# Softmax cross-entropy over 1 GB of logits: label logits picked out of the loaded tiles instead of gathered from memory

## The chip, the cores and the metric

The kernel runs on one core of one Trainium2 chip. The metric is the device time of one execution in microseconds, the median of several runs.

## The reference

```python
batch, seq, vocab = 16, 512, 32000          # logits float32, labels int32

def reference(logits, labels):
    logits_max = np.max(logits, axis=-1, keepdims=True)
    log_sum_exp = np.log(np.sum(np.exp(logits - logits_max), axis=-1)) + logits_max.squeeze(-1)
    log_probs = logits - log_sum_exp[..., np.newaxis]
    return -log_probs[np.arange(batch)[:, None], np.arange(seq), labels]
```

The loss of a row is log(sum(exp(row))) minus the row's logit at its label. The logits are 8192 rows of 32000 values, 1048.6 MB. All must be read once. From each row one single value, the label's logit, is needed besides the sum.

## The kernel before

The rows are laid out as 128 partitions times 64 groups, so one group is one row on each partition. Each group is loaded as two tiles of 128x16000 (8.2 MB each) into three rotating buffers. ScalarE (ACT) takes the exponential in place and sums it on the way. The label logits come by 64 indirect gathers, each fetching one 4-byte value per partition straight from HBM. GpSimd (POOL) issues them all at the start.

```python
    nc.gpsimd.iota(idx[:], pattern=[[V, G]], base=0, channel_multiplier=G * V)
    nc.gpsimd.tensor_tensor(out=idx[:], in0=idx[:], in1=labs32, op=ALU.add)
    for g in range(G):                      # G = 64
        nc.gpsimd.indirect_dma_start(
            out=lab_logit[:, g:g + 1], out_offset=None, in_=lg,
            in_offset=bass.IndirectOffsetOnAxis(ap=idx[:, g:g + 1], axis=1),
        )
    # ... (exp(g, ap): nc.scalar.activation(out=ap, in_=ap, func=EXP, accum_out=...))
    for j, (g, b, at, n) in enumerate(loads):
        if b not in buffers:
            buffers[b] = data.tile([P, W], FP32, tag="t", name="t")   # pool of 3 buffers, W = 16000
        t = buffers[b]
        # ...
        nc.sync.dma_start(out=t[:, at:at + n], in_=lg_pg[:, g, c0:c0 + n])
        exp(g, t[:, at:at + n])
        # ... (near the end: reduce the sums, logarithm, subtract lab_logit)
```

The first group and the last two are cut into smaller loads, so that the start and the end of the run are short.

The softmax here doesn't subtract the row's maximum and nothing guards it: scores larger than these inputs give would overflow.

Of the kernel before, what the change touches and what calls it, by code (L numbers as in the profile page):

```python
# [1 line left out]

# [5 lines left out]

FP32 = mybir.dt.float32  # L10
I32 = mybir.dt.int32


EXP = mybir.ActivationFunctionType.Exp
LN = mybir.ActivationFunctionType.Ln
ALU = mybir.AluOpType
X = mybir.AxisListType.X


@with_exitstack  # L20
def kernel(
    ctx: ExitStack,
    tc: tile.TileContext,
    logits: bass.AP,
    labels: bass.AP,
    out: bass.AP,
):
    nc = tc.nc

    B, S, V = logits.shape  # L30
    P = 128
    G = B * S // P
    W = 16000


    lg = logits.rearrange("b s v -> (b s) v")
    lg_pg = lg.rearrange("(p g) v -> p g v", g=G)
    labels_pg = labels.rearrange("b s -> (b s)").rearrange("(p g) -> p g", g=G)
    out_pg = out.rearrange("b s -> (b s)").rearrange("(p g) -> p g", g=G)



    loads = []

    def plan(g, widths_by_buffer, order):

        n_buffers = 1 + max((l[1] for l in loads), default=-1)
        for b, i in order:
            ws = widths_by_buffer[b]
            loads.append((g, n_buffers + b, sum(ws[:i]), ws[i]))  # L50

    plan(0, [[4000, 4000, 8000], [16000]], [(0, 0), (0, 1), (0, 2), (1, 0)])
    for g in range(1, G - 2):
        plan(g, [[W], [W]], [(0, 0), (1, 0)])
    plan(G - 2, [[W], [10000, 6000]], [(0, 0), (1, 0), (1, 1)])
    plan(
        G - 1,
        [[7400, 5840, 2260], [4540, 3720, 2920, 1780, 1460, 1120], [960]],
        [(0, 0), (0, 1), (1, 0), (1, 1), (1, 2), (0, 2), (1, 3), (1, 4), (1, 5), (2, 0)],
    )  # L60
    assert sum(l[3] for l in loads) == G * V

    data = ctx.enter_context(tc.tile_pool(name="data", bufs=3))
    persist = ctx.enter_context(tc.tile_pool(name="persist", bufs=1))

    labs64 = persist.tile([P, G], mybir.dt.int64)
    labs32 = labs64[:].bitcast(I32).rearrange("p (g two) -> p g two", two=2)[:, :, 0]
    idx = persist.tile([P, G], I32)
    lab_logit = persist.tile([P, G], FP32)
    K = 10  # L70
    sums = persist.tile([P, G - 1, 5], FP32)
    sums_last = persist.tile([P, K], FP32)
    totals = persist.tile([P, G - 1], FP32)
    logsum = persist.tile([P, G - 1], FP32)
    res = persist.tile([P, G - 1], FP32)
    part = persist.tile([P, 1], FP32)
    logsum_last = persist.tile([P, 1], FP32)
    res_last = persist.tile([P, 1], FP32)

    ctx.enter_context(tc.manual_schedule())  # L80


    nc.scalar.dma_start(out=labs64[:], in_=labels_pg)
    nc.scalar.preload_act_table_set("natural_log_exp_and_others")  # L84
    nc.vector.memset(sums[:], 0.0)  # L85
    nc.gpsimd.iota(idx[:], pattern=[[V, G]], base=0, channel_multiplier=G * V)  # L86
    nc.gpsimd.tensor_tensor(out=idx[:], in0=idx[:], in1=labs32, op=ALU.add)  # L87
    for g in range(G):
        nc.gpsimd.indirect_dma_start(  # L89
            out=lab_logit[:, g:g + 1],  # L90
            out_offset=None,
            in_=lg,
            in_offset=bass.IndirectOffsetOnAxis(ap=idx[:, g:g + 1], axis=1),
        )


    buffers = {}
    col = {}
    n_exp = {}

    def exp(g, ap):
        k = n_exp.get(g, 0)
        n_exp[g] = k + 1
        s = sums[:, g, k:k + 1] if g < G - 1 else sums_last[:, k:k + 1]
        nc.scalar.activation(out=ap, in_=ap, func=EXP, accum_out=s)  # L105

    for j, (g, b, at, n) in enumerate(loads):
        if b not in buffers:
            buffers[b] = data.tile([P, W], FP32, tag="t", name="t")
        t = buffers[b]  # L110
        c0 = col.get(g, 0)
        col[g] = c0 + n
        nc.sync.dma_start(out=t[:, at:at + n], in_=lg_pg[:, g, c0:c0 + n])  # L113
        exp(g, t[:, at:at + n])

        left = len(loads) - 1 - j
        if left == 6:
            nc.vector.reduce_sum(out=totals[:], in_=sums[:], axis=X)  # L118
        if left == 4:
            nc.scalar.activation(out=logsum[:], in_=totals[:], func=LN)  # L120
            nc.vector.tensor_tensor(out=res[:], in0=logsum[:], in1=lab_logit[:, 0:G - 1], op=ALU.subtract)  # L121
        if left == 1:
            nc.vector.reduce_sum(out=part[:], in_=sums_last[:, 0:K - 1], axis=X)  # L123
    assert n_exp[G - 1] == K
    nc.sync.dma_start(out=out_pg[:, 0:G - 1], in_=res[:])

    nc.scalar.activation(out=logsum_last[:], in_=sums_last[:, K - 1:K], func=LN, bias=part[:])  # L127
    nc.vector.tensor_tensor(out=res_last[:], in0=logsum_last[:], in1=lab_logit[:, G - 1:G], op=ALU.subtract)  # L128
    nc.sync.dma_start(out=out_pg[:, G - 1:G], in_=res_last[:])


# [1 line left out]
_INS = ['logits', 'labels']  # L133
_OUTS = [((16, 512), 'float32')]


# [23 lines left out]
```

## Time and profile before

| what | value |
|---|---|
| time, median of 3 runs | 2435.71 us |
| span of the profiled run | 2434.1 us |
| ACT busy | 1748.9 us (72%) |
| HBM read, mean rate | 1048.67 MB, 431 GB/s |
| full exp (128x16000) | 13.54 us |
| load of a full tile, issue to landing (median) | 43.0 us |

First, from the page: busy tenths and transfer rate in 40 slices of some 61 us, then the chain of waits.

```profile
ACT  4777766777677776777677776777667776777769
POOL 3222000000000000000000000000000000000000
DMA  9999999999999999999999999999999999999998
GB/s 421 422 421 433 425 438 431 427 438 438 433 426 436 438 434 426 435 438 434 426 435 436 435 430 431 436 435 430 431 436 438 431 427 436 438 433 426 438 433 377
...
DMA 76%; ACT 24%; issue 0%; SPq 0%; ACTq 0%; DVE 0%
```

The DMA engines are full from start to end, and nothing else is. POOL is busy only in the first four slices, where the gathers are. The chain is loads and, between them, the exps that free their buffers. The page's table of queues shows the two kinds of traffic; the columns are packets, MB and the share of the 16 engines' time. Below it is the page's line for the loads of full tiles, which ends with the median time from issue to landing (from the load's DMA instruction to the arrival of its last byte):

```profile
q1 hardware_dynamic: 20304, 1048.62, 99.8%
q0 software_dynamic: 2048, 0.04, 0.1%
...
t<-in_logits_dram SPq DMA_DIRECT2D x124, 8000.0 KB, 43.0
```

By its own time the gathers' queue (q0) seems not worth a thought. The windows view, by stretch of the run, shows more. Its columns are the stretch's length, the busy times of VectorE (DVE), ACT and POOL with instruction counts, the clock, the DMA share and the rate:

```profile
0.00:60.00 60.00, 0.32 (x1) 29.13 (x9) 19.68 (x26) 1.00 0.98 411
60.00:240.00 180.00, 0.00 (x0) 127.72 (x19) 39.44 (x42) 1.00 1.01 427
480.00:1200.00 720.00, 0.00 (x0) 517.89 (x76) 0.00 (x0) 1.00 1.00 433
```

While POOL issues gathers the loads move at 427 GB/s, afterwards at 433. The timeline shows the same in the starts of exps, first among gathers and then after them (start, duration, instruction, what ended the idle time before):

```profile
61.53 13.54 ACT L105 ACTIVATE t<-t 128x16000 f32<-128x16000 f32 x1 [5.79 <-DMA t<-in_logits_dram]
61.59 0.94 POOL L89 DMA_INDIRECT lab_logit<-in_logits_dram,idx  x1 [1.80 <-DMA lab_logit<-in_logits_dram,idx]
...
80.69 13.54 ACT L105 ACTIVATE t<-t 128x16000 f32<-128x16000 f32 x1 [5.52 <-DMA t<-in_logits_dram]
...
100.10 13.54 ACT L105 ACTIVATE t<-t 128x16000 f32<-128x16000 f32 x1 [5.78 <-DMA t<-in_logits_dram]
...
991.68 13.54 ACT L105 ACTIVATE t<-t 128x16000 f32<-128x16000 f32 x1 [5.27 <-DMA t<-in_logits_dram]
...
1010.60 13.54 ACT L105 ACTIVATE t<-t 128x16000 f32<-128x16000 f32 x1 [5.29 <-DMA t<-in_logits_dram]
```

Among gathers the exps start 19.16 and 19.41 us apart, later 18.92 us in the two lines shown and 18.89 to 18.91 us nearly everywhere. Each waits for its load, so these distances are the time of a load.

### The profile page before, as it was taken

To read this page: it belongs to the slowest core of one execution; us is meant where nothing else is said; L and a number is where in the kernel's file an instruction comes from. 1 tells how busy PE (TensorE), PEld (TensorE's weight loads), DVE (VectorE), ACT (ScalarE), POOL (GpSimd) and SP (SyncE) were. 2 spreads that over 40 slices of the span, in tenths; PEclk is the share of its full clock that TensorE was granted. 3 is DMA by queue.
4 is the path that set the end of the run, shared out by engine and by line. 5 is a ranking of instruction groups with operands and counts; after the bars stand their busy time and mean duration, and the time that the engine had idled before them with its cause. 6 is when DMAs were issued, how large, how long until landed. Compare 5 with 4: busy or idle time off the path is not lost.

```text
span 2434.1 us, 807 instructions
## 1 busy us (share of the span) xinstructions
DVE 1.3 (0%) x5; ACT 1748.9 (72%) x281; POOL 61.0 (3%) x70
## 2 busy tenths in 40 slices
DVE  0000000000000000000000000000000000000000
ACT  4777766777677776777677776777667776777769
POOL 3222000000000000000000000000000000000000
DMA  9999999999999999999999999999999999999998
GB/s 421 422 421 433 425 438 431 427 438 438 433 426 436 438 434 426 435 438 434 426 435 436 435 430 431 436 435 430 431 436 438 431 427 436 438 433 426 438 433 377
DMA packets 22502, 1048.77 MB, mean 431 GB/s; under 512 B 4576, under 2 KB 4704, under 8 KB 5216
## 3 DMA queue, kind: packets, MB, share of 16 engines
q1 hardware_dynamic: 20304, 1048.62, 99.8%
q0 software_dynamic: 2048, 0.04, 0.1%
q10 hardware_dynamic: 144, 0.07, 0.0%
q14 instruction: 6, 0.05, 0.0%
HBM read 1048.67 MB, written 0.03 MB: 431 GB/s over the span
## 4 chain that ended last, share of the span: by engine, by line
DMA 76%; ACT 24%; issue 0%; SPq 0%; ACTq 0%; DVE 0%
DMA t<-in_logits_dram 76%; ACT t L105 24%; SPq L113 0%; ACTq L105 0%; ACT logsum_last L127 0%; DVE res_last L128 0%; ACT logsum L120 0%
## 5 line engine op out<-in xcount | busy, mean ns | idle before, releaser
L105 ACT ACTIVATE t<-t 128x16000 f32<-128x16000 f32 (+5 forms) x139 | 1734.8, 12481 | 681.4 <-DMA t<-in_logits_dram 681.2
L89 POOL DMA_INDIRECT lab_logit<-in_logits_dram,idx x64 | 60.3, 942 | 178.3 <-DMA lab_logit<-in_logits_dram,idx 174.5
L105 ACT ACTIVATION_READ_ACCUMULATOR t<-t 128x1 f32 x139 | 25.9, 186 | 0.0
L84 ACT ACT_TABLE_LOAD x1 | 1.3, 1283 | 1.2 <-PEq L144 1.2
L118 DVE TENSOR_REDUCE totals<-sums 128x63 f32<-128x315 f32 x1 | 0.5, 480 | 2398.9 <-ACT t L105 2398.9
L87 POOL TENSOR_TENSOR idx<-idx,labs 128x64 int32<-128x64 int32 x1 | 0.3, 322 | 7.5 <-DMA labs<-in_labels_dram 7.5
L85 DVE MEMSET sums<- 128x315 f32 x1 | 0.3, 321 | 0.9 <-PEq L144 0.9
L127 ACT ACTIVATE logsum_last<-sums_last,part 128x1 f32<-128x1 f32 x1 | 0.3, 294 | 0.0
L121 DVE TENSOR_TENSOR res<-logsum,lab_logit 128x63 f32<-128x63 f32 x1 | 0.2, 225 | 25.3 <-ACT logsum L120 25.3
L120 ACT ACTIVATE logsum<-totals 128x63 f32<-128x63 f32 x1 | 0.2, 238 | 0.0
L86 POOL IOTA idx<- 128x64 int32 x1 | 0.2, 172 | 0.4 <-PEq L155 0.4
L123 DVE TENSOR_REDUCE part<-sums_last 128x1 f32<-128x9 f32 x1 | 0.2, 163 | 4.0 <-ACT t L105 4.0
L128 DVE TENSOR_TENSOR res_last<-logsum_last,lab_logit 128x1 f32<-128x1 f32 x1 | 0.2, 159 | 1.2 <-ACT logsum_last L127 1.2
L144 POOL MEMSET const-uint8-127<- 128x1 uint8 x1 | 0.1, 118 | 0.0
L144 POOL MEMSET const-bfloat16-1.0<- 128x1 bf16 x1 | 0.1, 113 | 0.0
L144 POOL MEMSET const-float32-0.0<- 128x1 f32 x1 | 0.1, 98 | 0.2 <-issue 0.2
L144 POOL MEMSET const-float32-1.0<- 128x1 f32 x1 | 0.1, 104 | 0.0
## 6 DMA issues: line engine op xcount, KB each, us to landing
t<-in_logits_dram SPq DMA_DIRECT2D x124, 8000.0 KB, 43.0
t<-in_logits_dram SPq DMA_DIRECT2D x1, 5000.0 KB, 35.9
t<-in_logits_dram SPq DMA_DIRECT2D x2, 2000.0 KB, 9.6
t<-in_logits_dram SPq DMA_DIRECT2D x1, 4000.0 KB, 21.4
t<-in_logits_dram SPq DMA_DIRECT2D x1, 3700.0 KB, 32.9
t<-in_logits_dram SPq DMA_DIRECT2D x1, 3000.0 KB, 42.6
t<-in_logits_dram SPq DMA_DIRECT2D x1, 2920.0 KB, 39.5
t<-in_logits_dram SPq DMA_DIRECT2D x1, 2270.0 KB, 26.4
```

Of the source, the lines that this page charges most:

```text
L84: nc.scalar.preload_act_table_set("natural_log_exp_and_others")
L85: nc.vector.memset(sums[:], 0.0)
L86: nc.gpsimd.iota(idx[:], pattern=[[V, G]], base=0, channel_multiplier=G * V)
L87: nc.gpsimd.tensor_tensor(out=idx[:], in0=idx[:], in1=labs32, op=ALU.add)
L89: nc.gpsimd.indirect_dma_start(out=lab_logit[:, g:g + 1], out_offset=None, in_=lg, in_offset=bass.IndirectOffsetOnAxis(ap=idx[:, g:g + 1], ...
L105: nc.scalar.activation(out=ap, in_=ap, func=EXP, accum_out=s)
L118: nc.vector.reduce_sum(out=totals[:], in_=sums[:], axis=X)
L120: nc.scalar.activation(out=logsum[:], in_=totals[:], func=LN)
L121: nc.vector.tensor_tensor(out=res[:], in0=logsum[:], in1=lab_logit[:, 0:G - 1], op=ALU.subtract)
L123: nc.vector.reduce_sum(out=part[:], in_=sums_last[:, 0:K - 1], axis=X)
L127: nc.scalar.activation(out=logsum_last[:], in_=sums_last[:, K - 1:K], func=LN, bias=part[:])
L144: nc = _bacc.Bacc("TRN2", target_bir_lowering=False, num_devices=1)
```

## The change

The intent: the label's logit passes through on-chip memory anyway with its tile, so it need not be fetched a second time. POOL's indexed copy takes 48 entries per tile out of it before the exp overwrites it. It returns 16 values on each partition for each column of its index list (3 columns and 48 values here). The program takes them as the picks of 16 neighbouring partitions, and VectorE sorts out each partition's own with a one-hot mask, four groups at a time. Groups 0, 61, 62 and 63 keep their gathers, three of them because their loads are cut in pieces.

```diff
+    gathered = [0, G - 3, G - 2, G - 1]
+    picked = [g for g in range(G) if g not in gathered]
-    for g in range(G):
+    for g in gathered:
         nc.gpsimd.indirect_dma_start(
 # ... about 25 small VectorE operations that make index lists and the one-hot mask, once
         nc.sync.dma_start(out=t[:, at:at + n], in_=lg_pg[:, g, c0:c0 + n])
+        if g in picked:
+            # ... (h: which half of the row; i: place in the batch of NB = 4; pk: tile of 128 x 8 x 48)
+            nc.gpsimd.indirect_copy(
+                out=pk[:, 2 * i + h, :], data=t[:], idxs=lists[:, g, h, 0:3], i_know_this_is_slow=True
+            )
         exp(g, t[:, at:at + n])
+        if g in picked and h == 1 and i == NB - 1:
+            nc.vector.copy_predicated(own[:], one_hot[:].unsqueeze(1).to_broadcast([P, NB * 2, NI]), pk[:])
+            nc.vector.reduce_sum(out=found[...], in_=own[...], axis=X)   # shortened
 # ... near the end: choose the half that holds the label, into lab_logit
```

More of the change, by code (lines that the diff above doesn't have):

```diff
@@ L64 @@
     persist = ctx.enter_context(tc.tile_pool(name="persist", bufs=1))
+    NI = 48
+    gathered = [0, G - 3, G - 2, G - 1]
+    picked = [g for g in range(G) if g not in gathered]
+    NB = 4
+    assert len(picked) % NB == 0
     labs64 = persist.tile([P, G], mybir.dt.int64)
@@ L69 @@
     lab_logit = persist.tile([P, G], FP32)
+    part16 = persist.tile([P, 1], I32)
+    part16f = persist.tile([P, 1], FP32)
+    mine = persist.tile([P, 3], FP32)
+    mine_at = persist.tile([P, 3], FP32)
+    at_entry = persist.tile([P, 1], FP32)
+    entries = persist.tile([P, NI], FP32)
+    one_hot = persist.tile([P, NI], mybir.dt.int32)
+    clamped = persist.tile([P, 2, G], FP32)
+    lists = persist.tile([P, G, 2, 4], mybir.dt.uint16)
+    own = persist.tile([P, NB * 2, NI], FP32)
+    found = persist.tile([P, 2, G], FP32)
+    in_first = persist.tile([P, G], mybir.dt.int32)
+    picks = ctx.enter_context(tc.tile_pool(name="picks", bufs=2))
     K = 10
@@ L87 @@
     nc.gpsimd.tensor_tensor(out=idx[:], in0=idx[:], in1=labs32, op=ALU.add)
-    for g in range(G):
+    nc.gpsimd.iota(part16[:], pattern=[[0, 1]], base=0, channel_multiplier=1)
+    nc.gpsimd.iota(entries[:], pattern=[[1, NI]], base=0, channel_multiplier=0, allow_small_or_imprecise_dtypes=True)
+    for g in gathered:
         nc.gpsimd.indirect_dma_start(
@@ L94 @@
         )
+    nc.vector.tensor_single_scalar(out=part16[:], in_=part16[:], scalar=15, op=ALU.bitwise_and)
+    nc.vector.tensor_copy(out=part16f[:], in_=part16[:])
+    for q in range(3):
+        nc.vector.tensor_scalar(
+            out=mine[:, q:q + 1], in0=part16f[:], scalar1=4.0 * q, scalar2=None, op0=ALU.add
+        )
+    for n in (12.0, 6.0):
+        nc.vector.tensor_scalar(
+            out=mine_at[:], in0=mine[:], scalar1=n, scalar2=n, op0=ALU.is_ge, op1=ALU.mult
+        )
+        nc.vector.tensor_tensor(out=mine[:], in0=mine[:], in1=mine_at[:], op=ALU.subtract)
+    nc.vector.tensor_scalar(out=mine[:], in0=mine[:], scalar1=4.0, scalar2=None, op0=ALU.is_ge)
+    for q in range(3):
+        nc.vector.tensor_scalar(
+            out=mine_at[:, q:q + 1], in0=mine[:, q:q + 1], scalar1=16.0 * q, scalar2=None, op0=ALU.mult
+        )
+    nc.vector.reduce_sum(out=at_entry[:], in_=mine_at[:], axis=X)
+    nc.vector.tensor_tensor(out=at_entry[:], in0=at_entry[:], in1=part16f[:], op=ALU.add)
+    nc.vector.tensor_scalar(
+        out=one_hot[:], in0=entries[:], scalar1=at_entry[:], scalar2=None, op0=ALU.is_equal
+    )
+    nc.vector.tensor_scalar(
+        out=clamped[:, 0, :], in0=labs32, scalar1=float(W - 1), scalar2=None, op0=ALU.min
+    )
+    nc.vector.tensor_scalar(
+        out=clamped[:, 1, :], in0=labs32, scalar1=float(-W), scalar2=0.0, op0=ALU.add, op1=ALU.max
+    )
+    nc.vector.tensor_scalar(
+        out=in_first[:], in0=labs32, scalar1=float(W), scalar2=None, op0=ALU.is_lt
+    )
+    for h in range(2):
+        for q in range(3):
+            nc.vector.tensor_scalar(
+                out=lists[:, :, h, q], in0=clamped[:, h, :], scalar1=mine[:, q:q + 1], scalar2=None, op0=ALU.mult
+            )
+    nc.vector.memset(own[:], 0.0)
     buffers = {}
@@ L113 @@
         nc.sync.dma_start(out=t[:, at:at + n], in_=lg_pg[:, g, c0:c0 + n])
-        exp(g, t[:, at:at + n])
+        if g in picked:
+            h = c0 // W
+            i = picked.index(g) % NB
+            if h == 0 and i == 0:
+                pk = picks.tile([P, NB * 2, NI], FP32, tag="pk", name="pk")
+            nc.gpsimd.indirect_copy(
+                out=pk[:, 2 * i + h, :], data=t[:], idxs=lists[:, g, h, 0:3], i_know_this_is_slow=True
+            )
+        exp(g, t[:, at:at + n])
+        if g in picked and h == 1 and i == NB - 1:
+            nc.vector.copy_predicated(own[:], one_hot[:].unsqueeze(1).to_broadcast([P, NB * 2, NI]), pk[:])
+            nc.vector.reduce_sum(
+                out=found[:, :, g - NB + 1:g + 1].rearrange("p h g -> p g h"),
+                in_=own[:].rearrange("p (g h) n -> p g h n", h=2),
+                axis=X,
+            )
         left = len(loads) - 1 - j
@@ L118 @@
             nc.vector.reduce_sum(out=totals[:], in_=sums[:], axis=X)
+            lo, hi = picked[0], picked[-1] + 1
+            nc.vector.tensor_copy(out=lab_logit[:, lo:hi], in_=found[:, 1, lo:hi])
+            nc.vector.copy_predicated(lab_logit[:, lo:hi], in_first[:, lo:hi], found[:, 0, lo:hi])
         if left == 4:
```

## The prediction

> **What bounds the kernel now.** The loads. The page shows DMA busy in every slice but the last at 9 tenths or more, 431 GB/s over the span; the windows view from 480 us on shows 433 GB/s. The chain of waits is 76% DMA of t and 24% exp. [...] ACT is busy 72%: an exp of 128x16000 takes 13.54 us, and in the timeline those start 18.90 us apart once things are steady, each waiting about 5.4 us for its load. A load lands 43.0 us after issue (median): 18.9 us of its own and about 24 us queued behind others.
>
> **What the change removes.** 60 of 64 indirect gathers. They run from 9 to 247 us on POOL, off the chain, but share the DMA engines: while they run, the twelve full exps after 42.1 us start 19.04 to 19.42 us apart, 231.2 us in all against 12 x 18.90 = 226.8 us, so 4.4 us lost. The first exp of a full tile, at 42.12 us, is by the same rate some 0.8 us late (first quarter tile landed at 8.3 us, started about 3.5 us, plus 37.8 us). Together about 5.2 us; 60/64 of it is about 4.9 us. This is the only gain, since the loads are unchanged.
>
> **What it adds.** (a) 120 indexed copies on POOL, each between the landing of a tile and its in-place exp. The trace has none. [...] (b) About 25 small VectorE operations once, 15 pairs of predicated copy and reduction (128x384, an estimate of 0.5 to 1 us each, from 0.48 us for the 128x315 reduction in this trace), and two at the end. All hide: VectorE is idle.
>
> **On the critical path?** The copy lengthens landing-to-release from 13.7 to 13.7 + x us, so the next load is issued x later and its queued time falls from 24 to 24 - x us. While x stays under roughly 18 us (and POOL under 18.9 us a tile) the DMA always holds another load and nothing is lost. [...] The last three groups are gathered, so the tail is as before.
>
> **Prediction.** 2435.7 - 4.9 = 2430.8 us; I say 2431, 2429 to 2434.5 with 8 in 10. Chances: faster by over 2% 0.01, within 2% 0.92, slower by over 2% 0.07.
>
> **What would show each step.** Right: exps start 18.90 us apart from about 60 us on instead of from 260 us; first slices at about 433 GB/s instead of 421; median issue-to-landing 43 minus x; the last 35 us unchanged; software DMA packets a sixteenth. Exps wait for POOL, not DMA.
>
> **What would make it wrong.** An indexed copy of over 18 us: POOL or the exchange of three buffers then paces the loads, and every microsecond over that costs about 120 us in all (at 25 us POOL alone needs 3000 us). A copy near 15 us would leave little queued and expose late engines, costing tenths of a microsecond per tile. The gathers' 19.3 us spacing may partly be a start-up effect unrelated to them; then the gain is under 4.9 us.

The sum of the forecast is 2435.7 - 4.9 = 2430.8 us, put as 2431 us; it had no term for a pick. x is the time of a pick, and "roughly 18 us" is the estimate, set below the 24 us that a load queues. The "late engines" have this ground in the trace of the kernel before: the 16 landings recorded for each full load lie 0.6 to 2.4 us apart (median 1.3 us). That they would cost tenths of a microsecond per tile was a guess, which runs below test.

## The result

The changed kernel takes 2431.28 us (median of 4 runs, 2431.22 to 2431.33), the kernel before beside it 2435.61 us. The ratio is 0.9982, with a 95% interval of 0.9965 to 0.9999. The outputs are right. The change is a gain of 4.3 us. The span of the profiled run fell from 2434.1 to 2429.5 us, by 4.6 us.

The page after, the same lines:

```profile
ACT  4777767777677767777677776777667776777769
POOL 0000000000000000000000000000000000000000
DMA  9999999999999999999999999999999999999998
GB/s 423 438 423 437 438 428 432 438 436 424 438 436 428 434 438 433 427 438 435 429 434 437 433 428 437 435 427 435 437 434 429 435 437 426 435 437 433 430 434 377
...
q1 hardware_dynamic: 20304, 1048.62, 99.8%
...
q0 software_dynamic: 128, 0.00, 0.0%
...
DMA 73%; ACT 24%; issue 2%; POOL 1%; SPq 0%; POOLq 0%; DVE 0%; ACTq 0%
```

The gathers' queue is down to a sixteenth. A single slice of the GB/s row says little, since all slices but the last scatter between 423 and 438. The windows view averages enough to see it:

```profile
0.00:60.00 60.00, 4.35 (x27) 29.13 (x9) 5.04 (x12) 1.00 1.00 427
60.00:240.00 180.00, 1.15 (x2) 130.55 (x19) 6.81 (x10) 1.00 1.00 433
480.00:1200.00 720.00, 5.74 (x10) 519.06 (x77) 25.82 (x38) 1.00 1.00 434
```

The stretch from 60 to 240 us now has the rate of the rest of the run, 433 GB/s. The timeline after has the pick between landing and exp:

```profile
61.36 0.69 POOL L182 INDIRECT_COPY pk<-t,lists 128x48 f32 x1 [46.96 <-DMA t<-in_logits_dram]
62.08 13.54 ACT L168 ACTIVATE t<-t 128x16000 f32<-128x16000 f32 x1 [6.81 <-POOL pk L182]
...
80.24 0.69 POOL L182 INDIRECT_COPY pk<-t,lists 128x48 f32 x1 [18.20 <-DMA t<-in_logits_dram]
80.96 13.54 ACT L168 ACTIVATE t<-t 128x16000 f32<-128x16000 f32 x1 [5.25 <-POOL pk L182]
...
99.79 13.54 ACT L168 ACTIVATE t<-t 128x16000 f32<-128x16000 f32 x1 [5.20 <-POOL pk L182]
```

The exps start 18.88 and 18.83 us apart here, without the slow start. They wait for POOL now, but ACT's wait before each exp is no longer than it was later in the run before. The page's groups of new work (busy time, mean ns of one) and its first line of DMA issues:

```profile
L182 POOL INDIRECT_COPY pk<-t,lists 128x48 f32 x120 | 81.6, 680 | 2216.8 <-DMA t<-in_logits_dram 2216.8
L187 DVE COPY_PREDICATED own<-one_hot,pk 128x384 f32<-128x384 int32 x15 | 8.9, 593 | 2282.9 <-POOL pk L182 2282.9
...
L188 DVE TENSOR_REDUCE found<-own 128x8 f32<-128x384 f32 x15 | 8.3, 555 | 0.5
...
t<-in_logits_dram SPq DMA_DIRECT2D x124, 8000.0 KB, 41.6
```

Issue to landing is 41.6 us, where it was 43.0: the loads are issued 1.4 us later and spend that much less time queued. The pick therefore lengthens the path from landing to release by 1.4 us, twice the 0.68 us that its line shows. This will matter below.

Where the gain lies can be read from the starts of corresponding exps in the two timelines. Exp 4 (the first full tile, no pick in front of it) starts at 42.12 us before and 41.64 us after, 0.48 us earlier. Exp 18 starts at 311.24 and 307.71 us, 3.53 us earlier though it now has a pick of about 1.4 us in front, so its tile landed some 4.9 us earlier. From there on nothing more is gained: exp 125, the first without a pick again, starts at 2334.94 and 2330.34 us, 4.60 us earlier. Between them one lone spacing of 19.24 us (exp 21 to 22), which the kernel before has not in that place, gives back 0.3 us. To the end the difference stays 4.6 us, so the tail is as it was.

### The profile page after: what moved, and what is told of

Same layout as the page of the kernel before. It is cut to its first block, busy times and chain, and to the rows that moved or that the text cites. A ratio compares the mean times of both kernels' runs of the same rounds, so it can differ in the third digit from the quotient of the medians. Undisturbed runs are those within 1.5% of the kernel's fastest.

```text
span 2429.5 us, 954 instructions
## 1 busy us (share of the span) xinstructions
DVE 22.9 (1%) x63; ACT 1748.9 (72%) x281; POOL 86.6 (4%) x132
## 4 chain that ended last, share of the span: by engine, by line
DMA 73%; ACT 24%; issue 2%; POOL 1%; SPq 0%; POOLq 0%; DVE 0%; ACTq 0%
DMA t<-in_logits_dram 73%; ACT t L168 24%; POOL pk L182 1%; SPq L176 0%; POOLq L236 0%; ACT logsum_last L208 0%; DVE res_last L209 0%; ACT logsum L201 0%; POOLq L182 0%; ACTq L168 0%
## 5 line engine op out<-in xcount | busy, mean ns | idle before, releaser
L182 POOL INDIRECT_COPY pk<-t,lists 128x48 f32 x120 | 81.6, 680 | 2216.8 <-DMA t<-in_logits_dram 2216.8
L187 DVE COPY_PREDICATED own<-one_hot,pk 128x384 f32<-128x384 int32 x15 | 8.9, 593 | 2282.9 <-POOL pk L182 2282.9
L188 DVE TENSOR_REDUCE found<-own 128x8 f32<-128x384 f32 x15 | 8.3, 555 | 0.5
L114 POOL DMA_INDIRECT lab_logit<-in_logits_dram,idx x4 | 4.1, 1033 | 1.2 <-issue 0.9
## 6 DMA issues: line engine op xcount, KB each, us to landing
t<-in_logits_dram SPq DMA_DIRECT2D x124, 8000.0 KB, 41.6
```

Source lines behind the costliest of these rows:

```text
L114: nc.gpsimd.indirect_dma_start(out=lab_logit[:, g:g + 1], out_offset=None, in_=lg, in_offset=bass.IndirectOffsetOnAxis(ap=idx[:, g:g + 1], ...
L182: nc.gpsimd.indirect_copy(out=pk[:, 2 * i + h, :], data=t[:], idxs=lists[:, g, h, 0:3], i_know_this_is_slow=True)
L187: nc.vector.copy_predicated(own[:], one_hot[:].unsqueeze(1).to_broadcast([P, NB * 2, NI]), pk[:])
L188: nc.vector.reduce_sum(out=found[:, :, g - NB + 1:g + 1].rearrange("p h g -> p g h"), in_=own[:].rearrange("p (g h) n -> p g h n", h=2), a ...
```

## The experiments

The theory: the gathers' small transfers slow the loads by about 0.08 us for each gather of 128 values, wherever in the run they are, and the picks cost nothing because they fit in the queued time of the loads. The rivals: (A) the picks give back part of a larger gain; (B) the later issue of loads is what helps, not the missing gathers; (C) the slow first 250 us are a start-up effect. The first four runs below shared one chip, where the kernel before took 2435.74 us; the next two shared a second (before 2435.75 us), the last three a third (before 2435.78 us).

### Neither gathers nor picks

The kernel before with the gather loop taken out. Its output is wrong, which doesn't matter for the time.

```diff
-    for g in range(G):
-        nc.gpsimd.indirect_dma_start(...)
+    nc.vector.memset(lab_logit[:], 0.0)
```

> The kernel before without any gather and without any pick (label logits set to zero, so a wrong result on purpose). Theory (the gathers' traffic slows the loads by about 5 us, picks cost nothing): 5.2 us under before, about 2430.5 us, so at most 0.5 us under the change. Rival A (the picks cost some of what the gathers gave back): clearly under the change, 2 us or more. Rival B (the picks' delaying of the loads' issue is what helps, not the missing gathers): as before, 2435.6 us.

Measured: 2430.81 us, 0.5 us under the change (0.6 us when each is set against the kernel before in its own session: 4.9 against 4.3 us gained). Its exp 4 starts at 41.38 us, 0.74 us earlier than before, and the spacing is 18.90 us from there on but for single longer ones. Its windows view:

```profile
60.00:240.00 180.00, 0.00 (x0) 132.23 (x19) 0.00 (x0) 1.00 1.00 432
```

So the picks and the four remaining gathers together cost about half a microsecond, and rivals A and B fall. This also bounds what a version without any gather could still gain.

### Picks and gathers both

The change with its 60 gathers added back, two behind each pick of groups 1 to 15 (issued in the loop; in the kernel before, POOL was busy with its gathers until 247 us, so 60 of them ahead of the first pick would have held it up).

```diff
+        if g in picked and g <= 15:
+            for gg in picked[4 * (g - 1) + 2 * h:4 * (g - 1) + 2 * h + 2]:
+                nc.gpsimd.indirect_dma_start(out=lab_logit[:, gg:gg + 1], ...)
         exp(g, t[:, at:at + n])
```

> The change with its 120 picks, and the 60 gathers back as well, two behind each pick of groups 1 to 15; their values are overwritten by the picks, so the result is right. Theory: the loss comes back whole, since there are 64 gathers again: about 2431.3 + 4.9 = 2436 us, spread over some 600 us with exps about 19.05 to 19.1 us apart there. Rival B (the delayed issue helps): 2431 us. Rival C (a start-up effect, not the gathers): 2431 us.

Measured: 2435.60 us, as before; the result is right. The whole gain is gone although all picks are there. The exps of the 30 tiles with gathers start mostly 19.03 to 19.08 us apart, then 18.90 us. With 64 gathers each, the kernel with picks (2435.60) and that without (2435.74) take the same time: the picks cost nothing that can be seen within the scatter of about half a microsecond. B falls again, and so does C.

### Twice the gathers

```diff
-    for g in range(G):
+    for g in list(range(G)) * 2:
         nc.gpsimd.indirect_dma_start(
```

> The kernel before with every gather issued twice (128 gathers, right result). Theory: the loss is in proportion to the gathers, 0.08 us each: about 2435.6 + 5.2 = 2441 us, with exps about 19.3 us apart until about 490 us. Rival C (start-up effect): 2435.6 us.

Measured: 2440.47 us, 4.7 us more. The windows view of this run shows the slow rate lasting twice as long:

```profile
60.00:240.00 180.00, 0.00 (x0) 127.63 (x19) 39.59 (x42) 1.00 1.01 427
240.00:480.00 240.00, 0.00 (x0) 172.20 (x26) 52.80 (x56) 1.00 1.01 427
600.00:1200.00 600.00, 0.00 (x0) 435.61 (x64) 0.00 (x0) 1.00 1.00 434
```

With 0, 64 and 128 gathers the times are 2430.81, 2435.74 and 2440.47 us: 0.077 and 0.074 us for each gather, a straight line as far as three points can show it.

### The gathers late

All 64 gathers moved into the loop behind the exp of load 60; a small POOL copy that reads this exp's sum holds them back.

```diff
-    for g in range(G):
-        nc.gpsimd.indirect_dma_start(...)
 # ... in the loop of loads:
         exp(g, t[:, at:at + n])
+        if j == 60:
+            nc.gpsimd.tensor_copy(out=gate[:], in_=sums[:, g, 0:1])
+            for gg in range(G):
+                nc.gpsimd.indirect_dma_start(out=lab_logit[:, gg:gg + 1], ...)
```

> The kernel before with all 64 gathers held back until the exp of load 60, about 1.1 ms into the run (right result). Theory: the loss moves with them: 18.90 us spacing at the start, about 19.3 us from 1.1 to 1.35 ms, total unchanged at 2435.6 us. Rival C (the slow first 250 us are a start-up effect): the slow spacing stays at the start and the total is 2435.6 us or more with none at 1.1 ms.

Measured: 2435.99 us, as before. The windows view of this run:

```profile
60.00:240.00 180.00, 0.00 (x0) 132.12 (x19) 0.00 (x0) 1.00 1.00 432
1120.00:1330.00 210.00, 0.00 (x0) 149.07 (x22) 49.39 (x53) 1.00 1.01 427
1400.00:2300.00 900.00, 0.00 (x0) 646.11 (x97) 0.00 (x0) 1.00 1.00 433
```

The slow stretch moved with the gathers; in it most exps start 19.06 to 19.44 us apart. Rival C falls.

### Gathers that all read one place

The kernel before with indices that name the same place in every gather, the start of each partition's rows, instead of the labels' places. Its output is wrong, which doesn't matter for the time.

```diff
-    nc.gpsimd.iota(idx[:], pattern=[[V, G]], base=0, channel_multiplier=G * V)
-    nc.gpsimd.tensor_tensor(out=idx[:], in0=idx[:], in1=labs32, op=ALU.add)
+    nc.gpsimd.iota(idx[:], pattern=[[0, G]], base=0, channel_multiplier=G * V)
```

> The kernel before with its 64 gathers all reading the same place of each partition's rows instead of the labels' (wrong result on purpose): as many descriptors, no scattered reads of HBM. If the loss comes from the number of small transfers in the DMA engines: as before, 2435.6 us, exps 19.3 us apart until 250 us. If it comes from scattered HBM reads disturbing the loads: toward 2431 us.

Measured: 2435.66 us, as before, with the same spacings of 19.1 and 19.4 us and the same rate:

```profile
60.00:240.00 180.00, 0.00 (x0) 127.34 (x19) 36.90 (x39) 1.00 1.01 427
```

It does not matter that the labels are scattered over 1 GB; 128 places read 64 times over cost as much. The price goes with the small transfers, wherever they read. What POOL does to issue them was not separated from the packets they send; that POOL is merely busy is not the cause, since in a run below its copies fill 17.5 of every 18.9 us at no cost. The packet records of the trace say where: in the kernel before, the load packets of 64,000 bytes took 2398 ns on average between 60 and 240 us and 2365 ns between 500 and 2000 us; in the changed kernel 2365 ns in both. Summed over all engines, the load packets took 38,860.7 us before and 38,805.1 us after, and the gathers' own packets 24.4 us and 1.5 us. That is 55.6 + 22.9 = 78.5 us over 16 engines, or 4.9 us for each. By these records about three tenths of the loss is the gathers' own packets, and seven tenths is load packets made longer beside them. The split is rough, for the recorded times of packets overlap a little (the DMA share reads 1.01 among gathers), and the profiled runs differ by 4.6 us and not 4.9. Not every load packet suffers: of those that start between 60 and 240 us in the kernel before, 521 take about 2366 ns, as later in the run, and 664 about 2424 ns. In that time 1335 packets of gathers started, two for each gather and engine (2048 for 64 gathers on the page). So each gather lengthens about one load packet on each of the 16 engines, by some 58 ns. Why a load packet gets longer was not tried.

### How long a pick takes, and how much room there is

The change with one more indexed copy behind each pick, from the same tile into an unused one. Results stay right, and each exp waits longer.

```diff
+        if g in picked:
+            nc.gpsimd.indirect_copy(out=spare[:], data=t[:], idxs=zeros[:], i_know_this_is_slow=True)  # 480 entries
         exp(g, t[:, at:at + n])
```

> The change with one more indexed copy behind each pick, of 480 entries (all of index 0) into an unused tile, so the result stays right and each exp waits c longer. It measures c: about 6.8 us if a copy's 0.68 us grows with its entries, about 0.7 us if it is mostly fixed[...]. Theory (slack of some 18 us): with c of 7 us the issue to landing falls from 41.6 to about 35 us, the spacing stays 18.90 us, the time stays 2431.3 us. Rival (any lengthening between landing and release costs time): 120 x c = over 800 us more.

Measured: 2431.14 us, as the change. My guess at c was a miss. Issue to landing fell from 41.6 to 30.7 us, so the copy takes 10.9 us, where the expectation allowed for 6.8 or 0.7. The timeline of this run shows why the guess misled:

```profile
80.21 0.70 POOL L185 INDIRECT_COPY pk<-t,lists 128x48 f32 x1 [7.25 <-DMA t<-in_logits_dram]
...
90.50 1.26 POOL L190 INDIRECT_COPY spare<-t,zeros 128x480 f32 x1 [9.59 <-issue]
91.79 13.54 ACT L171 ACTIVATE t<-t 128x16000 f32<-128x16000 f32 x1 [5.17 <-POOL spare L190]
```

The second copy is shown as 1.26 us long, but POOL had nothing else to do from the end of the first at 80.91 us. So the 9.59 us "issue" before it belong to it, 10.85 us in all, and the fall of issue to landing by 10.9 us says the same. The span that the profile shows for an indexed copy is thus only a part of its time: 1.26 us of 10.85 here, and 0.68 us of about 1.4 us for the pick. The whole came from the ends of consecutive instructions on POOL for the one, and from issue to landing for the other.

Three longer copies look for the edge. Below, x is the whole time that pick and second copy put between landing and exp.

```diff
-    spare = persist.tile([P, 480], FP32)     # and zeros with 30 columns
+    spare = persist.tile([P, 624], FP32)     # 39 columns; in the other two runs 720 (45) and 816 (51)
```

> As e6_long_x1 with 624 entries in the second copy. From 1.4 us for 48 and 10.9 us more for 480 (issue to landing fell from 43.0 to 41.6 and to 30.7): about 0.022 us an entry, so x = 15.5 us from landing to the exp. Theory (slack of some 18 us): still 2431.3 us, issue to landing 27.5 us. Rival (the prediction's own worry: near 15 us little is queued and late DMA engines cost tenths of a microsecond a tile): 2445 us or more.

> As before with 720 entries: x = 17.6 us, POOL nearly full (18.9 us a tile). Theory: still 2431 to 2432 us, issue to landing 25.4 us. Rival (late engines): tens of microseconds more.

> As before with 816 entries: x = 19.7 us, more than the 18.9 us of a load. Theory: POOL paces the loads at 19.7 us a tile; 120 x 0.8 = 96 us more, less what the head start of the loads absorbs, so 2500 to 2530 us, slower by 3 to 4%. If it stays at 2431 us the slack is not set by POOL and the account of x is wrong.

| entries of the second copy | its time (end of the first copy to its own end) | issue to landing | time |
|---|---|---|---|
| none (the change) | | 41.6 us | 2431.28 us |
| 480 | 10.85 us | 30.7 us | 2431.14 us |
| 624 | 14.01 us | 27.6 us | 2431.22 us |
| 720 | 16.13 us | 25.4 us | 2431.17 us |
| 816 | 18.23 us | 21.4 us | 2516.00 us |

The row of 720 from its timeline, and then that of 816:

```profile
1007.06 0.70 POOL L185 INDIRECT_COPY pk<-t,lists 128x48 f32 x1 [2.08 <-DMA t<-in_logits_dram]
...
1022.43 1.46 POOL L190 INDIRECT_COPY spare<-t,zeros 128x720 f32 x1 [14.67 <-issue]
```

```profile
1003.07 0.70 POOL L185 INDIRECT_COPY pk<-t,lists 128x48 f32 x1 [0.66 <-issue]
...
1020.46 1.54 POOL L190 INDIRECT_COPY spare<-t,zeros 128x816 f32 x1 [16.70 <-issue]
1022.03 13.54 ACT L171 ACTIVATE t<-t 128x16000 f32<-128x16000 f32 x1 [5.96 <-POOL spare L190]
1022.65 0.70 POOL L185 INDIRECT_COPY pk<-t,lists 128x48 f32 x1 [0.65 <-issue]
```

With 720 entries POOL still waits for the landing of each tile (the 2.08 us), and the time is that of the change to a tenth of a microsecond, although landing to release is 16 us longer. The rival worry about late DMA engines is refuted here, up to these 17.5 us of pick and copy. With 816, after the first tile no pick waits for a load: pick and second copy take 19.58 us a tile, more than the 18.90 us of a load, and exps start 19.58 or 19.59 us apart, except for one longer by about 0.25 us in eight, that of the copy during which VectorE sorts the picks of four groups. About 119 spacings times 0.69 us plus fifteen times 0.25 us is 86 us; measured were 2516.00 - 2431.28 = 84.7 us. The edge is POOL's throughput, where the theory had it.

The windows view of the run with 816 entries holds a warning:

```profile
480.00:1200.00 720.00, 6.22 (x10) 498.28 (x75) 83.20 (x74) 1.00 1.00 418
```

POOL sets the pace here, and the rate is 418 GB/s against 434 for the change. Yet the share of the DMA engines still reads 1.00 and the page's DMA row still shows nines. The packet records tell why the share hides it: one in eight of the 64,000-byte packets (590 of 4704 in this stretch) takes over 2.4 us, with a median of 2.98 us, where in the change nearly all take 2.37 us. A full DMA row alone does not show that the DMA engines are the limit.

From 480 to 816 entries the copy grows by 7.38 us, or 0.022 us an entry, which leaves 0.31 us fixed. For the 48 entries of the change this gives 1.36 us, and the issue-to-landing times gave 1.4 us.

## Why the prediction was right

The prediction was 2431.0 us, within 2429.0 to 2434.5; measured were 2431.28 us. Point by point:

- **What bounds the kernel.** Right. The loads do, in both kernels. Where loads run alone they move at 433 GB/s (480 to 1200 us of the kernel before) with a DMA share of 1.00.
- **What the gathers cost.** Right in mechanism and size. About 5.2 us were predicted for 64; the runs with 0 and 64 gathers differ by 4.9 us. Moved gathers moved the loss, doubled gathers doubled it, and added back they brought it back. The caveat that the slow start might have been a start-up effect is refuted.
- **The gain.** 4.9 us predicted, 4.3 us measured between medians. The timelines show 4.9 us gained by exp 18, and then the lone 19.24 us spacing that costs 0.3 us and leaves 4.6 us. The rest is scatter between runs: the profiled run of the kernel before took 2435.88 us, 0.3 us above the median of 2435.61 us. Single longer spacings turn up in every run, with and without gathers; an instruction fetch in the DMA records lies near this one (at 377.3 us), but the kernel before also has one (at 382.7 us) without the delay. Its cause stays open.
- **What a pick costs.** Mis-sized by a factor of three, without effect on the time; that it did no harm is owed to the room that the queued loads leave, not to the estimate. The estimate rested on no trace or run of this case. Measured were 1.4 us for the 48 entries: 0.022 us an entry and 0.31 us fixed. How the copy spends this time inside was not shown.
- **That it hides.** Right. Landing to release may grow by 17.5 us (pick plus 720 entries) with nothing lost, and the limit is reached between 17.5 and 19.6 us. What was reached is the second of the two limits predicted, "POOL under 18.9 us a tile". The first, that the queue of loads runs out at "roughly 18 us", was not seen on its own: no run lengthens landing to release without also filling POOL. The fear that 15 us would already cost tenths of a microsecond per tile was wrong: at 15.4 us (pick plus 624 entries) the time was 2431.22 us.
- **VectorE.** 15 pairs at 0.59 and 0.56 us, inside the 0.5 to 1 us estimated, and hidden.
- **What the profile would show.** Spacing of 18.90 us from about 60 us on, waits for POOL in place of DMA, an issue to landing of 43 less x, a sixteenth of the software packets, an unchanged tail: all there. One sign was badly chosen: "first slices at 433 instead of 421" cannot be read from single slices, which scatter by some 15 GB/s; the windows view shows it as 427 against 433.

## What to carry to other kernels

In this kernel, whose loads fill the DMA engines (433 GB/s, share 1.00), 64 small gathers cost 4.9 us although nothing waited for them, and about seven tenths of it was not their own packet time: in a kernel of this kind, measure the spacing of the big loads with and without such transfers before calling them free. Work that goes between a load's landing and the release of its buffer was free here up to 17.5 us a tile, with the load queue filled and POOL needing less time per tile than the 18.90 us of a load; at 19.58 us on POOL it cost 84.7 us in all. Before building such a change, work out the whole prize: here it was 5 us of 2436, and the change got nearly all of it.
